# Ordering the tail of each feed-forward part, and a different reduction in the last norm

## The chip, the cores and the metric

The kernel runs on one core of one Trainium2 chip. The metric is the device time of one execution in microseconds (us). Engines in the profile: PE is TensorE's matmuls, PEld its weight loads, DVE is VectorE, ACT is ScalarE, POOL is GpSimd, SP issues the DMAs.

## The reference

Two layers of a bidirectional encoder on a sequence of 512 tokens of width 1024 in float32. Each layer has three sublayers, so six in all, numbered n = 0 to 5 here: feed-forward, mixer (a state-space scan in layer 0, attention in layer 1), feed-forward.

```python
for i in range(DEPTH):                                   # DEPTH = 2
    mods = (silu(c) @ ada_w[i] + ada_b[i]).reshape(b, 3, 3, D_MODEL)
    gate = lambda s: (1 + mods[:, s, 2])[:, None, :]
    y = swiglu(modulate(x, mods[:, 0]), w_gate[i, 0], w_up[i, 0], w_down[i, 0])
    x = layer_norm(ALPHA * x + 0.5 * gate(0) * y, ln_g[i, 0], ln_b[i, 0])
    y = mixer(modulate(x, mods[:, 1]))
    x = layer_norm(ALPHA * x + gate(1) * y, ln_g[i, 1], ln_b[i, 1])
    y = swiglu(modulate(x, mods[:, 2]), w_gate[i, 1], w_up[i, 1], w_down[i, 1])
    x = layer_norm(ALPHA * x + 0.5 * gate(2) * y, ln_g[i, 2], ln_b[i, 2])
# swiglu(u) = (silu(u @ w_gate) * (u @ w_up)) @ w_down, hidden width 2816
# layer_norm: (x - mean) / sqrt(var + 1e-5) * g + b over the 1024 features
```

## The kernel before

Activations lie transposed: 128 features on the partitions, 512 tokens along the free axis, so the residual `res[0..7]` is eight tiles. Each float32 value is held as a high part and a low part (`hi`/`lo`, `uh`/`ul` for activations, `wh`/`wl` for weights), and each product is three matmuls: high by high, high by low, low by high (`mm3`, L182). A weight tile is loaded as `raw` (512 KB, or 448 KB for a down tile of seven blocks), ACT copies it to `wh` (L123) and DVE subtracts to get `wl` (L126). There are five `raw` buffers in all during a feed-forward sublayer (four of the tag `raw` and one of the tag `raw5`), and all loads are issued from SP's queue at L99.

A feed-forward sublayer (`ffn`) splits its 22 hidden tiles into three parts of 8, 7 and 7. In a part, each hidden tile is computed, and then eight down units (`down_units`), one for each output tile, multiply the part's hidden tiles by a down weight (`wdn`) and add to the residual (`add_res`, L415, output `resid`). The hidden tiles come in two ways. Up to tile `first7` (10 for n = 0, 4 for the others) both projections are plain. From then on `seven` computes both by seven products of half blocks in place of eight (Strassen's scheme), from `input_forms` (sums of input halves) and `weight_forms` (sums of weight blocks, L543, L544 and L553). Its last product is `product(3, ...)` into the tile `mid`; behind it come, in a chain, L590 (`px`, DVE), L591 (`sg`, ACT: SiLU), L592 (`sg`, DVE), and `split_act`, which writes `hi` (L155, ACT) and `lo` (L156, DVE). A down unit multiplies the part's hidden tiles in their order, so the last hidden tile is needed by the last eighth (or seventh) of unit 0.

The modulation vectors (`mods`) are computed on DVE from another set of weights: a modulation unit (`ada_unit`, L207) loads one `raw` tile `in_adaw` and multiplies it by the conditioning vector with a running sum. Layer 0's units run in `ffn(0)`, layer 1's in `ffn(2)` and `ffn(3)`; `advance(stream, per[...])` issues two of them after each down unit in the first two parts of these three sublayers, one in the last part of `ffn(0)`, none in the last parts of the other two, and none at all in `ffn(5)`.

Nothing in the code fixes the order of the work of one engine except the data, the manual dependencies (`add_manual_dep` with `NOSYNC`: the one instruction stands behind the other on the engine's queue) and a scheduler, which plays the program forward when the kernel is built, and writes each engine's queue: of the instructions that are ready in its own model, the one that the program issues first goes first. On the chip each queue is then fixed.

The norm (`LN`) of the sublayers keeps two running sums on DVE, `sc` of the residual tiles and `ss` of their squares (`feed`, L326, L328, L329). `stats` reduces them over the partitions with matmuls by constant tiles (L335 for the broadcast mean in `mid`, L339 for mean and mean square by token), forms the variance on DVE (L344, L346, L349), takes the power -1/2 on POOL (L353), spreads the result by transposes (L276) and subtracts the mean from pairs of residual tiles (L357). `normalize` then scales; for the last norm, n = 5, it writes tile by tile on DVE (L367) and ACT (L370) and issues the output DMAs by pairs of tiles. The last four output tiles of the last part are done in two halves of 256 tokens, and the first half's normalization runs beside the second half's matmuls (`finish`).

Of the kernel before, what the change touches and what calls it, by code (L numbers as in the profile page):

```python
# [9 lines left out]
F32 = mybir.dt.float32  # L10
F32R = mybir.dt.float32r
AF = mybir.ActivationFunctionType
ALU = mybir.AluOpType

P = 128
# [31 lines left out]
def hybrid_trunk(tc, xT, cb, par, cst, adaw, wgu, wdn0, wdn1, wdn2, wdt, win, wso, wqk, wv, wao, dist_in, dtp, lam_in, out):  # L47
# [39 lines left out]
    def pc(c, n=1):  # L87
        return pars[:, c : c + n]


    fifth, at, last_load, hold_split = [None], [0], [None], [None]

    def load(src, n=1024):
        at[0] = (at[0] + 1) % 5
# [12 lines left out]
    def split(raw, where=None, home=None):  # L107

        n = raw.shape[-1]
        if where == "a":  # L110
            hi, lo = [], []
            for o in range(0, n, T):
                r = raw[:, o : o + T]
                h, l = big(F32R, "wah"), big(F32R, "wal")
                x = nc.scalar.activation(h, r, AF.Copy)
                y = nc.vector.tensor_tensor(out=l, in0=r, in1=h.bitcast(F32), op=ALU.subtract)
                for a, b in zip((x, y), behind):
                    tc.add_manual_dep(a.ins, b.ins.name, NOSYNC, reason="inputs before weights")
                hi.append(h)
                lo.append(l)  # L120
            return [(hi[c // T][:, c % T : c % T + P], lo[c // T][:, c % T : c % T + P]) for c in range(0, n, P)]
        hi, lo = ring(home)
        x = nc.scalar.activation(hi[:, :n], raw, AF.Copy)  # L123
        if hold_split[0] is not None:
            tc.add_manual_dep(x.ins, hold_split[0].ins.name, NOSYNC, reason="decay matrices first")
        nc.vector.tensor_tensor(out=lo[:, :n], in0=raw, in1=hi[:, :n].bitcast(F32), op=ALU.subtract)  # L126
        return Unit(hi, lo, n)

    def ring(home=None):
# [17 lines left out]

    def split_act(src, scale=None):
        hi, lo = big(F32R, "hi"), big(F32R, "lo")
        split_into(hi, lo, src, scale)  # L150
        return hi, lo

    def split_into(hi, lo, src, scale=None):
        if scale is None:
            x = nc.scalar.activation(hi, src, AF.Copy)  # L155
            y = nc.vector.tensor_tensor(out=lo, in0=src, in1=hi.bitcast(F32), op=ALU.subtract)  # L156
            return x, y
        else:
            nc.scalar.activation(hi, src, AF.Copy, scale=scale)
            nc.vector.scalar_tensor_tensor(  # L160
                out=lo, in0=src, scalar=scale, in1=hi.bitcast(F32), op0=ALU.mult, op1=ALU.subtract
            )
# [41 lines left out]

    def ada_unit(l, j):
        raw = load(adaw[l, j])
        nc.vector.scalar_tensor_tensor(  # L207
            out=raw, in0=raw, scalar=1.0, in1=cond, op0=ALU.mult, op1=ALU.mult,
            accum_out=mods[l][:, j : j + 1],
        )  # L210

    onep, shift, gvec, lnG, lnB, lnag, lnab = {}, {}, {}, {}, {}, {}, {}

# [84 lines left out]
    class LN:  # L298


        def __init__(self, n):
            self.n = n
            self.u = None

        def shift(self):

# [11 lines left out]
        def feed(self, d, a, b):  # L318
            z = res[d][:, a:b]
            if d == 0:  # L320
                self.sc = ap.tile([P, T], F32, tag="l", name="sc", bufs=3)
                self.ss = ap.tile([P, T], F32, tag="l", name="ss", bufs=3)
                nc.scalar.activation(self.ss[:, a:b], z, AF.Square)
                return
            sq = sp.tile([P, T], F32, tag="sq", name="sq")
            nc.scalar.activation(sq[:, a:b], z, AF.Square)  # L326
            c0 = res[0] if d == 1 else self.sc
            nc.vector.tensor_tensor(out=self.sc[:, a:b], in0=c0[:, a:b], in1=z, op=ALU.add)  # L328
            nc.vector.tensor_tensor(out=self.ss[:, a:b], in0=self.ss[:, a:b], in1=sq[:, a:b], op=ALU.add)  # L329

        def stats(self, a, b):
            n, m = self.n, (b - a) // P
            st = acc("ln")
            mb = acc("mid")[:, : b - a]
            nc.tensor.matmul(mb, lhsT=onesd, rhs=self.sc[:, a:b], start=True, stop=True)  # L335
            for q, c0 in enumerate((self.sc, self.ss)):
                for j in range(m):
                    o = a + j * P
                    nc.tensor.matmul(  # L339
                        st[:, q * m + j : q * m + j + 1], lhsT=c0[:, o : o + P], rhs=invd, start=True, stop=True  # L340
                    )
            rb = acc("ln")[:, : b - a]
            sv = sp.tile([P, 4], F32, tag="sv", name="sv")
            nc.vector.tensor_copy(sv[:, :m], st[:, :m])  # L344
            vr = sp.tile([P, 4], F32, tag="vr", name="vr")
            nc.vector.scalar_tensor_tensor(  # L346
                out=vr[:, :m], in0=sv[:, :m], scalar=-1.0, in1=sv[:, :m], op0=ALU.mult, op1=ALU.mult
            )
            ready = nc.vector.scalar_tensor_tensor(  # L349
                out=vr[:, :m], in0=st[:, m : 2 * m], scalar=EPS, in1=vr[:, :m], op0=ALU.add, op1=ALU.add  # L350
            )
            r = sp.tile([P, 4], F32, tag="rr", name="rr")
            nc.gpsimd.tensor_tensor(out=r[:, :m], in0=vr[:, :m], in1=mhalf[:, :m], op=ALU.pow)  # L353
            bcast_cols(rb, r[:, :m])
            for d in range(0, KT, 2):
                pair = resid[:, d : d + 2, a:b]
                x = nc.vector.tensor_tensor(out=pair, in0=pair, in1=two(mb), op=ALU.subtract)  # L357
                if d:
                    tc.add_manual_dep(x.ins, ready.ins.name, NOSYNC, reason="variance first")
            return rb  # L360

        def normalize(self, a, b, rb):
            n = self.n
            if n == 5:
                for d in range(KT):
                    t = res[d][:, a:b]
                    nc.vector.scalar_tensor_tensor(  # L367
                        out=t, in0=t, scalar=pc(C_LNG + n * 8 + d), in1=rb, op0=ALU.mult, op1=ALU.mult
                    )
                    nc.scalar.activation(t, t, AF.Identity, bias=pc(C_LNB + n * 8 + d))  # L370
                    if d % 2:
                        nc.sync.dma_start(
                            out[(d - 1) * P : (d + 1) * P, a:b].rearrange("(e p) t -> p e t", e=2),
                            resid[:, d - 1 : d + 1, a:b],
                        )
                    yield
                return
            if self.u is None:
# [217 lines left out]
    def ffn(n, stream=None, per=(0, 0, 0), pre=None, first7=FT):  # L596
# [10 lines left out]
        for pi, nf in enumerate(FPARTS):  # L607
# [36 lines left out]
            def mk(d):  # L644
                return lambda: [(d, split(load(wdn[pi][idx, d], nf * P)))]

            for _ in down_units(n, hs, [mk(d) for d in range(KT)], ln if pi == len(FPARTS) - 1 else None):
                advance(stream, per[1 if pi < 2 else 2])
            if pi == len(FPARTS) - 2:
                shifting = ln.shift()  # L650
        extra[0] = fifth[0] = None
# [746 lines left out]
```

## Time and profile before

| what | value |
|---|---|
| median of 3 runs | 2131.68 us (2131.55 to 2135.46) |
| the profiled execution: its time, its span | 2134.65 us, 2132.8 us |
| TensorE's granted clock in it | 0.997 |
| busy in the span: PE, PEld | 2099.9 us (98%), 1854.1 us (87%) |
| busy in the span: DVE, ACT, POOL | 1770.3 us (83%), 1093.8 us (51%), 180.6 us (8%) |
| mean traffic of the DMA engines | 141 GB/s |

In a timeline row stand the start in us from the span's start, the duration in us, engine, line of the kernel, operation, output and inputs by the program's names, shape and count, and in brackets the idle time of the engine just before it with what ended it. In a row of waits stand the engine and what waited, what it waited for, then the total in us, the number of times and the longest. In a row of stages stand the stretch, its length, the busy time of each engine, the clock, the DMA share and GB/s. In a row of groups stand the count, the busy time in us, the mean duration of one in ns, and the idle time before them.

### The profile page before, as it was taken

The page shows a single profiled execution, that of the slowest core. Times are in us where ns is not written, and L with a number is a line of the kernel's source. Part 1 is how long each engine was busy: PE and PEld are TensorE (multiplying, and loading weights), DVE is VectorE, ACT ScalarE, POOL GpSimd, SP SyncE. Part 2 cuts the span into 40 slices and gives each one's busy share as a digit, 9 for nine tenths or more (in the row PEclk, how much of TensorE's full clock was granted, in tenths as well). Part 3 has the DMA queues.
Part 4 walks back from the last instruction along what each step waited for, and adds up shares of the span by engine and source line. Part 5 has one row for each costly group of instructions (what it writes and reads, how often), then busy time and mean ns, then how long its engine had stood idle before and what let it go on. Part 6 is the DMA issues. An engine that isn't in the chain of part 4 may idle for free.

```text
span 2132.8 us, 34111 instructions
## 1 busy us (share of the span) xinstructions
PE 2099.9 (98%) x13234; PEld 1854.1 (87%) x13234; DVE 1770.3 (83%) x2932; ACT 1093.8 (51%) x1833; POOL 180.6 (8%) x258
## 2 busy tenths in 40 slices
PE   7999999999999999999999999999999999999998
PEld 6889899976777699899999989899988888989897
DVE  6979998677667898989988989997788889858796
ACT  5424354777656646343456434353866647424343
POOL 0000000056333400000000000000011100000000
PEclk9999999999999999999999999999999999999999
DMA  8863735375554352727343373723322322323231
GB/s 321 306 227 99 247 97 195 93 214 170 151 152 135 92 159 72 271 91 238 123 144 104 106 240 103 253 96 113 92 69 80 90 81 78 124 75 119 71 118 40
DMA packets 90274, 301.19 MB, mean 141 GB/s; under 512 B 10240, under 2 KB 13696, under 8 KB 90112
## 3 DMA queue, kind: packets, MB, share of 16 engines
q1 hardware_dynamic: 88576, 294.81, 42.6%
q0 software_dynamic: 1536, 4.20, 0.9%
q8 instruction: 104, 1.70, 0.3%
q14 instruction: 58, 0.48, 0.1%
HBM read 289.53 MB, written 5.24 MB: 138 GB/s over the span
## 4 chain that ended last, share of the span: by engine, by line
PE 85%; DVE 7%; DMA 2%; issue 2%; ACT 2%; POOL 1%; SPq 0%; POOLq 0%; ACTq 0%; DVEq 0%
PE acc L182 68%; PE mid L182 9%; PE mid L909 2%; PE mid L1142 1%; DVE raw L207 1%; PE ln L182 1%; DMA raw<-in_adaw 1%; DVE raw L553 1%; DVE wl L544 1%; DMA raw<-in_wdn 1%; PE ln L1164 1%; PE ln L847 0%; POOL E L899 0%; DVE wl L126 0%; PE ln L339 0%
## 5 line engine op out<-in xcount | busy, mean ns | idle before, releaser
L182 PE MATMUL acc<-hi,wh 128*128 128x256 f32 (+1 forms) x1568 | 522.0, 334 | 1.8 <-ACT hi L155 1.8
L182 PE MATMUL acc<-lo,wh 128*128 128x256 f32 (+1 forms) x1568 | 521.8, 333 | 0.6 <-DVE lo L156 0.6
L182 PE MATMUL acc<-hi,wl 128*128 128x256 f32 (+1 forms) x1568 | 520.6, 333 | 0.0
L182 PE MATMUL acc<-uh,wh 128*128 128x256 f32 (+1 forms) x1160 | 391.7, 339 | 0.0
L182 PE MATMUL acc<-uh,wl 128*128 128x256 f32 (+1 forms) x1160 | 386.6, 335 | 0.0
L182 PE MATMUL acc<-ul,wh 128*128 128x256 f32 (+1 forms) x1160 | 384.0, 335 | 0.0
L123 ACT ACTIVATE wh<-raw 128x1024 fp32r<-128x1024 f32 (+1 forms) x210 | 212.4, 1022 | 278.3 <-PE acc L182 109.6
L543 ACT ACTIVATE wh<-raw 128x1024 fp32r<-128x1024 f32 x198 | 209.3, 1059 | 255.2 <-DVE raw L553 115.2
L182 PEld LDWEIGHTS acc<-hi,wh 128*128 128x128 f32 x1568 | 295.9, 189 | 35.9 <-ACT hi L155 5.2
L182 PEld LDWEIGHTS acc<-lo,wh 128*128 128x128 f32 x1568 | 296.3, 189 | 31.0 <-DVE lo L156 2.4
L182 PEld LDWEIGHTS acc<-hi,wl 128*128 128x128 f32 x1568 | 296.0, 189 | 29.2
L126 DVE TENSOR_TENSOR wl<-raw,wh 128x1024 fp32r<-128x1024 f32 (+1 forms) x210 | 248.4, 1188 | 49.3 <-ACT wh L123 46.7
L544 DVE TENSOR_TENSOR wl<-raw,wh 128x1024 fp32r<-128x1024 f32 x198 | 240.9, 1219 | 22.5 <-ACT wh L543 21.0
L182 PEld LDWEIGHTS acc<-uh,wh 128*128 128x128 f32 x1160 | 219.1, 189 | 28.3 <-issue 6.4
L182 PEld LDWEIGHTS acc<-uh,wl 128*128 128x128 f32 x1160 | 219.1, 189 | 22.7 <-issue 0.4
L182 PEld LDWEIGHTS acc<-ul,wh 128*128 128x128 f32 x1160 | 217.5, 189 | 21.9 <-issue 0.6
L553 DVE TENSOR_TENSOR raw<-raw 128x512 f32<-128x512 f32 x264 | 181.3, 688 | 4.9
L207 DVE SCALAR_TENSOR_TENSOR raw<-raw,cond 128x1024 f32<-128x1024 f32 x144 | 173.7, 1218 | 10.5 <-DMA raw<-in_adaw 10.3
L415 DVE SCALAR_TENSOR_TENSOR resid<-acc,gv,resid 128x512 f32<-128x512 f32 (+1 forms) x156 | 104.5, 672 | 82.7 <-PE acc L182 82.1
L353 POOL TENSOR_TENSOR rr<-vr,mhalf 128x2 f32<-128x2 f32 x12 | 8.4, 698 | 1515.6 <-DVE vr L349 1515.6
L182 PE MATMUL mid<-uh,wh 128*128 128x256 f32 (+2 forms) x332 | 99.2, 301 | 0.5 <-DVE up L585 0.5
L182 PE MATMUL mid<-uh,wl 128*128 128x256 f32 (+2 forms) x332 | 99.0, 299 | 0.0
(268 smaller groups left out, 3926.0 us busy)
## 6 DMA issues: line engine op xcount, KB each, us to landing
raw<-in_wgu SPq DMA_DIRECT2D x176, 512.0 KB, 4.0
raw<-in_adaw SPq DMA_DIRECT2D x144, 512.0 KB, 4.7
raw<-in_wdn SPq DMA_DIRECT2D x64, 448.0 KB, 4.1
raw<-in_win SPq DMA_DIRECT2D x40, 512.0 KB, 4.0
raw<-in_wdn SPq DMA_DIRECT2D x32, 512.0 KB, 4.5
rw<-scr SPq DMA_DIRECT2D x32, 512.0 KB, 6.0
ch<-scr SPq DMA_DIRECT2D x32, 256.0 KB, 6.2
raw<-in_wso SPq DMA_DIRECT2D x16, 512.0 KB, 4.3
```

Source lines behind the costliest of these rows:

```text
L123: x = nc.scalar.activation(hi[:, :n], raw, AF.Copy)
L126: nc.vector.tensor_tensor(out=lo[:, :n], in0=raw, in1=hi[:, :n].bitcast(F32), op=ALU.subtract)
L182: last = nc.tensor.matmul(o, lhsT=a, rhs=b, start=start and j == 0, stop=j == len(pairs) - 1, skip_group_check=not start)
L207: nc.vector.scalar_tensor_tensor(out=raw, in0=raw, scalar=1.0, in1=cond, op0=ALU.mult, op1=ALU.mult, accum_out=mods[l][:, j : j + 1],)
L353: nc.gpsimd.tensor_tensor(out=r[:, :m], in0=vr[:, :m], in1=mhalf[:, :m], op=ALU.pow)
L415: nc.vector.scalar_tensor_tensor(out=res[d][:, a:b], in0=pd[:, a:b], scalar=gvec[n][:, d : d + 1], in1=res[d][:, a:b], op0=ALU.mult, op1=A ...
L543: nc.scalar.activation(x[0], r, AF.Copy)
L544: nc.vector.tensor_tensor(out=x[1], in0=r, in1=x[0].bitcast(F32), op=ALU.subtract)
L553: nc.vector.tensor_tensor(out=o, in0=x, in1=y, op=ALU.add)
L909: x = nc.tensor.matmul(py[hh * 64 : (hh + 1) * 64, cc], lhsT=lhs, rhs=rhs, start=k == 0, stop=k == 2)
L1142: nc.tensor.matmul(ss[m], lhsT=q[:, c], rhs=qks[h, 1][m], start=j == 0, stop=j == 1)
L1164: gated(nc.tensor.transpose(pw[:, k * P : (k + 1) * P], w[:, k * P : (k + 1) * P], ident))
```

## The change

It has three parts.

1. `split_act` remembers the two instructions of the latest activation split (`last_act`). In each of the three parts of each feed-forward sublayer, after down unit 0 has been issued, `part_end` is set to them until three units later: the ACT copy and the DVE subtraction of the splits of down units 1, 2 and 3, and the DVE multiplication of the modulation units issued after down units 0, 1 and 2, are ordered behind the two.
2. In the second half of the last norm (n = 5), the last residual tile is no longer added to `sc` and its square no longer to `ss`. TensorE adds them in the accumulation of the mean and of the token columns, each as a second matmul, with the column groups of the squares in a bank of their own and the broadcast mean's second matmul last.
3. In the same norm `normalize` multiplies pairs of residual tiles by the root in one DVE instruction, the gain moves into the ACT instruction (as its scale, with the bias as before), and in the second half the last three tiles get gain and bias on DVE (`tensor_scalar`).

```diff
+    last_act, part_end = [None], [None]
+
+    def behind_part(*xs):
+        for x, y in zip(xs, part_end[0] or ()):
+            tc.add_manual_dep(x.ins, y.ins.name, NOSYNC, reason="last activations of the part first")
...
     def split(raw, where=None, home=None):
...
-        nc.vector.tensor_tensor(out=lo[:, :n], in0=raw, in1=hi[:, :n].bitcast(F32), op=ALU.subtract)
+        y = nc.vector.tensor_tensor(out=lo[:, :n], in0=raw, in1=hi[:, :n].bitcast(F32), op=ALU.subtract)
+        behind_part(x, y)
         return Unit(hi, lo, n)
...
     def split_act(src, scale=None):
         hi, lo = big(F32R, "hi"), big(F32R, "lo")
-        split_into(hi, lo, src, scale)
+        last_act[0] = split_into(hi, lo, src, scale)
...
     def ada_unit(l, j):
         raw = load(adaw[l, j])
-        nc.vector.scalar_tensor_tensor(
+        x = nc.vector.scalar_tensor_tensor(
             out=raw, in0=raw, scalar=1.0, in1=cond, op0=ALU.mult, op1=ALU.mult,
             accum_out=mods[l][:, j : j + 1],
         )
+        if part_end[0]:
+            tc.add_manual_dep(x.ins, part_end[0][1].ins.name, NOSYNC, reason="last activations of the part first")
...
         def feed(self, d, a, b):
...
             nc.scalar.activation(sq[:, a:b], z, AF.Square)
+            if self.n == 5 and d == KT - 1 and a:
+                self.ends = (res[d], sq)
+                return
...
         def stats(self, a, b):
-            nc.tensor.matmul(mb, lhsT=onesd, rhs=self.sc[:, a:b], start=True, stop=True)
-            for q, c0 in enumerate((self.sc, self.ss)):
+            s2 = acc() if self.ends else st[:, m:]
+            cs, ss = ((x,) + self.ends[q : q + 1] for q, x in enumerate((self.sc, self.ss)))
+
+            def mean(i):
+                nc.tensor.matmul(mb, lhsT=onesd, rhs=cs[i][:, a:b], start=i == 0, stop=i == len(cs) - 1)
+
+            mean(0)
+            for to, c in ((st, cs), (s2, ss)):
+                prev = None
                 for j in range(m):
                     o = a + j * P
-                    nc.tensor.matmul(
-                        st[:, q * m + j : q * m + j + 1], lhsT=c0[:, o : o + P], rhs=invd, start=True, stop=True
-                    )
+                    for i, c0 in enumerate(c):
+                        x = nc.tensor.matmul(
+                            to[:, j : j + 1], lhsT=c0[:, o : o + P], rhs=invd, start=i == 0, stop=i == len(c) - 1
+                        )
+                        if prev is not None and self.ends:
+                            tc.add_manual_dep(x.ins, prev.ins.name, NOSYNC, reason="one accumulation group per bank")
+                        prev = x
+            if len(cs) > 1:
+                mean(1)
...
         def normalize(self, a, b, rb):
             if n == 5:
-                for d in range(KT):
-                    t = res[d][:, a:b]
-                    nc.vector.scalar_tensor_tensor(
-                        out=t, in0=t, scalar=pc(C_LNG + n * 8 + d), in1=rb, op0=ALU.mult, op1=ALU.mult
-                    )
-                    nc.scalar.activation(t, t, AF.Identity, bias=pc(C_LNB + n * 8 + d))
...
+                for d in range(0, KT, 2):
+                    pair = resid[:, d : d + 2, a:b]
+                    nc.vector.tensor_tensor(out=pair, in0=pair, in1=two(rb), op=ALU.mult)
+                    for e in range(2):
+                        t, G, B = res[d + e][:, a:b], pc(C_LNG + n * 8 + d + e), pc(C_LNB + n * 8 + d + e)
+                        if b == T and d + e > 4:
+                            nc.vector.tensor_scalar(out=t, in0=t, scalar1=G, scalar2=B, op0=ALU.mult, op1=ALU.add)
+                        else:
+                            nc.scalar.activation(t, t, AF.Identity, bias=B, scale=G)
+                    nc.sync.dma_start(out[d * P : (d + 2) * P, a:b].rearrange("(e p) t -> p e t", e=2), pair)
...
     def ffn(n, stream=None, per=(0, 0, 0), pre=None, first7=FT):
-            for _ in down_units(n, hs, [mk(d) for d in range(KT)], ln if pi == len(FPARTS) - 1 else None):
+            ends = last_act[0]
+            for i, _ in enumerate(down_units(n, hs, [mk(d) for d in range(KT)], ln if pi == len(FPARTS) - 1 else None)):
+                part_end[0] = ends if i < 3 else None
                 advance(stream, per[1 if pi < 2 else 2])
+            part_end[0] = None
```

More of the change, by code (lines that the diff above doesn't have):

```diff
@@ L303, in __init__ @@
             self.u = None
+            self.ends = ()
         def shift(self):
@@ L349, in stats @@
             ready = nc.vector.scalar_tensor_tensor(
-                out=vr[:, :m], in0=st[:, m : 2 * m], scalar=EPS, in1=vr[:, :m], op0=ALU.add, op1=ALU.add
+                out=vr[:, :m], in0=s2[:, :m], scalar=EPS, in1=vr[:, :m], op0=ALU.add, op1=ALU.add
             )
@@ L364, in normalize @@
             if n == 5:
-                for d in range(KT):
-                    t = res[d][:, a:b]
-                    nc.vector.scalar_tensor_tensor(
-                        out=t, in0=t, scalar=pc(C_LNG + n * 8 + d), in1=rb, op0=ALU.mult, op1=ALU.mult
-                    )
[L370 to L375, printed above, removed]
+                for d in range(0, KT, 2):
[8 more added lines that the diff above has]
+                    nc.sync.dma_start(out[d * P : (d + 2) * P, a:b].rearrange("(e p) t -> p e t", e=2), pair)
+                    yield
                     yield
```

## The prediction

> **What bounds the kernel now.** I read the page's busy row first, then the list of waits of TensorE, to see what a change at the ends of the feed-forward parts can win.
>
> ```profile
> PE 2099.9 (98%) x13234; PEld 1854.1 (87%) x13234; DVE 1770.3 (83%) x2932; ACT 1093.8 (51%) x1833; POOL 180.6 (8%) x258
> ...
> PE acc L182 <- ACT wah L115: 11.4, 1, 11.4
> ...
> PE acc L182 <- ACT hi L155: 1.8, 3, 0.8
> ...
> PE acc L182 <- DVE lo L156: 0.6, 1, 0.6
> ```
>
> TensorE is the bound: 98% of a span of 2132.8 us, and the largest wait (11.4 us) is the start, which the change leaves alone. The waits that the ties aim at are the last two rows: three times for `hi` (L155), once for `lo` (L156), 2.4 us in all. One of the four, with VectorE around it, shows the mechanism (timeline of DVE, of ACT, of PE; columns are start, duration, then the instruction):
>
> ```profile
> 871.18 1.21 DVE L126 TENSOR_TENSOR wl<-raw,wh 128x1024 fp32r<-128x1024 f32 x1
> ...
> 878.20 1.23 DVE L126 TENSOR_TENSOR wl<-raw,wh 128x1024 fp32r<-128x1024 f32 x1 [0.75 <-ACT wh L123]
> 879.34 1.22 DVE L207 SCALAR_TENSOR_TENSOR raw<-raw,cond 128x1024 f32<-128x1024 f32 x1
> 880.48 0.42 DVE L590 TENSOR_TENSOR px<-px,mid 128x256 f32<-128x256 f32 x1
> 880.82 1.22 DVE L126 TENSOR_TENSOR wl<-raw,wh 128x1024 fp32r<-128x1024 f32 x1
> 881.95 0.68 DVE L592 TENSOR_TENSOR sg<-sg,up 128x512 f32<-128x512 f32 x1
> 882.55 1.22 DVE L207 SCALAR_TENSOR_TENSOR raw<-raw,cond 128x1024 f32<-128x1024 f32 x1
> 883.70 0.68 DVE L156 TENSOR_TENSOR lo<-sg,hi 128x512 fp32r<-128x512 f32 x1
> 884.30 1.21 DVE L207 SCALAR_TENSOR_TENSOR raw<-raw,cond 128x1024 f32<-128x1024 f32 x1
> 885.45 0.74 DVE L415 SCALAR_TENSOR_TENSOR resid<-acc,gv,resid 128x512 f32<-128x512 f32 x1
> 886.11 1.21 DVE L126 TENSOR_TENSOR wl<-raw,wh 128x1024 fp32r<-128x1024 f32 x1
> ...
> 879.65 1.06 ACT L123 ACTIVATE wh<-raw 128x1024 fp32r<-128x1024 f32 x1 [0.54 <-DMA raw<-in_wdn]
> 880.93 0.42 ACT L591 ACTIVATE sg<-px 128x256 f32<-128x256 f32 x1 [0.22 <-DVE px L590]
> 882.67 0.63 ACT L155 ACTIVATE hi<-sg 128x512 fp32r<-128x512 f32 x1 [1.31 <-DVE sg L592]
> ...
> 878.60 0.28 PE L182 MATMUL mid<-uh,wl 128*128 128x256 f32 x1
> 878.72 0.39 PE L182 MATMUL acc<-hi,wl 128*128 128x512 f32 x1
> ...
> 882.38 0.40 PE L182 MATMUL acc<-hi,wh 128*128 128x512 f32 x1
> 882.62 0.39 PE L182 MATMUL acc<-lo,wh 128*128 128x512 f32 x1
> 883.35 0.50 PE L182 MATMUL acc<-hi,wh 128*128 128x512 f32 x1 [0.34 <-ACT hi L155]
> ```
>
> The last Strassen product of the part starts its last matmul at 878.60. Behind it come L590, L591, L592, L155, L156 one after the other, and two modulation units (L207) and two splits (L126) of the down weights stand among them on VectorE. Without them the five take 0.42 + 0.42 + 0.68 + 0.63 + 0.68 = 2.83 us and some 0.2 us of hand-offs: `lo` would end 0.3 + 3.0 = 3.3 us behind 878.60, at 881.9, in place of 884.4. So the diagnosis behind the ties is true: 2.5 us of delay on a short chain. TensorE hides all but 0.7 us of it under the first seven eighths of down unit 0.
>
> **What the ties win.** The rows call 2.4 us idle. From start to start 883.35 - 882.62 is 0.73 us where neighbours are 0.24 apart (882.62 - 882.38), so 0.49 are lost where the row says 0.34. Scaling 2.4 by 0.49/0.34 gives 3.5 us, which I take; the ends are 2.4 and 3.5. (The Trainium skill, "Perfetto Trace Analysis", section "Tensor Engine Instruction (MATMUL, LD_WEIGHTS)", says that a matmul's end is an estimate and only its start is observed; by that rule starts count and the win is 3.5, by the rows as they stand 2.4. These three rows agree with the rule.)
>
> **What the ties cost.** A part's splits 1 to 3 (`wh` behind the last `hi` on ACT, `wl` behind the last `lo` on DVE) and the modulation units that follow units 0, 1, 2 now all queue behind the chain. Nothing orders them among themselves but the program, in which the two units issued after down unit 0 come before split 1. The kernel's scheduler keeps to that order among what is ready: at 884.30 above it takes a modulation unit before a split whose `wh` was done at 880.71 (split 4, at 886.11). At the end of the last `lo` both units' data have long landed, while split 1's `wh` begins on ACT only behind `hi` and takes 1.06 us, longer than `lo`. So I expect DVE: `lo`, modulation unit, modulation unit, `wl` of split 1. From start to start a unit takes 1.14 (879.34 to 880.48), so `wl` ends 2 x 1.14 + 1.22 = 3.5 us after `lo`, and 0.74 later still if unit 0's `resid` (L415) slips in.
>
> When does TensorE need it? After 878.72 sixteen matmuls of 0.232 remain before the last eighth: its first at 882.43, the one with `lo` at 882.66, 0.76 us after `lo` would end. Then two of that unit and two of unit 1 (each 0.232), and the next needs `wl`: 0.93 later. The slack is 0.76 + 0.93 = 1.7 us, the delay 3.5: a new stall of 1.8 us in this part, where split 1 was finished at 872.4 before. A part of seven tiles has 21 matmuls a unit in place of 24: 0.7 us less, stall 2.5.
>
> Five parts end on Strassen products and have two units after each down unit: layer 0's first feed-forward part 2 of 3 (seven tiles), parts 1 (eight) and 2 (seven) of the sublayers n=2 and n=3. That is 2 x 1.8 + 3 x 2.5 = 11.1 us. The last part of n=0 has one unit per down unit: 1.14 + 1.22 - 1.0 = 1.4. Ends for these six: nothing if split 1 goes first, and 6 x 3.5 = 21 if there is no slack.
>
> The first part of n=0 is of another kind: there the last `split_act` is not an activation but the second half of `input_forms`, which is needed only later:
>
> ```profile
> 103.46 0.68 DVE L631 TENSOR_TENSOR h<-sg,acc 128x512 f32<-128x512 f32 x1
> ...
> 106.20 1.22 DVE L126 TENSOR_TENSOR wl<-raw,wh 128x1024 fp32r<-128x1024 f32 x1
> ...
> 112.22 0.69 DVE L156 TENSOR_TENSOR lo<-fb,hi 128x512 fp32r<-128x512 f32 x1
> ```
>
> From `h` (103.46) to the end of that `lo` (112.91) are 9.45 us, in which two units, one split and one `resid` take some 4.3. Taken out, `lo` ends at 108.6; units and split 1 to 112.1. TensorE's unit 1 starts at about 108.1 and needs `wl` 0.5 later: 3.5 us, or less if `h` moves up too. I take 3.0 (ends 0 and 4.2, with `resid`).
>
> Parts without modulation units (last part of n=2 and n=3, all of n=5) queue only split 1: `wh` ends 1.06 after `hi`, `wl` 1.2 later, 1.6 after `lo`, against 1.0 to 1.7 of slack: I take 0 (ends 0 and 0.6 x 5 = 3). What covers them is that slack alone.
>
> **Behind the stalls: VectorE and the loads.**
>
> ```profile
> 865.00:884.00 19.00, 18.66 (x133) 17.21 (x133) 18.11 (x30) 8.54 (x12) 0.00 (x0) 1.00 0.75 244
> 884.00:925.00 41.00, 41.00 (x190) 33.93 (x189) 34.81 (x52) 11.00 (x12) 0.00 (x0) 1.00 0.65 234
> ...
> 861.47 3.61 SPq L99 DMA_DIRECT2D raw<-in_wdn  x2
> ...
> 898.11 6.16 SPq L99 DMA_DIRECT2D raw<-in_wgu  x5
> ```
>
> (Columns of the first two rows: length, busy PE, PEld, DVE, ACT, POOL, clock, DMA share, GB/s.) DVE is full ahead of the chain (18.1 of 19 us) because units and splits run ahead; that work, four units and two splits in that window (7.3 us) and three more units before it (3.6), moves behind. The down stage has 41 - 34.8 = 6.2 us idle for these 10.9. Loads wait likewise: all five `raw` buffers hold tied data, SP's queue stops on the next buffer, and loads that ran from 861 on start after the first unit is through. In place of 898 the next part's `in_wgu` go perhaps 10 us later. The eight down units of 24 matmuls last 44.5 us on TensorE, to about 927, so I put this at 0, with 8 us (two for each of four following parts) as the other end.
>
> **The last norm.** Its tail, in order:
>
> ```profile
> 2120.15 0.28 PE L182 MATMUL acc<-hi,wl 128*128 128x256 f32 x1
> 2121.72 0.70 PE L335 MATMUL mid<-sc,onesd 128*128 128x256 f32 x2 [1.30 <-DVE sc L328]
> 2122.62 0.58 PE L339 MATMUL ln<-invd,ss 128*128 128x1 f32 x4
> ...
> 2124.10 0.16 DVE L349 SCALAR_TENSOR_TENSOR vr<-ln,vr 128x2 f32<-128x2 f32 x1
> 2124.18 1.87 DVE L357 TENSOR_TENSOR resid<-resid,mid 128x512 f32<-128x512 f32 x3
> 2125.97 3.22 DVE L367 SCALAR_TENSOR_TENSOR resid<-resid,pars,ln 128x256 f32<-128x256 f32 x8
> 2126.48 3.30 ACT L370 ACTIVATE resid<-resid,pars 128x256 f32<-128x256 f32 x8 [3.54 <-DVE resid L367]
> ...
> L339 PE MATMUL ln<-invd,ss 128*128 128x1 f32 x48 | 6.9, 247 | 0.0
> L382 DVE TENSOR_TENSOR resid<-resid,ln 128x512 f32<-128x512 f32 x40 | 25.9, 678 | 0.2 <-PE ln L276 0.2
> L706 DVE TENSOR_SCALAR E<-E 128x256 f32<-128x256 f32 x1 | 0.3, 294 | 1.4 <-ACT E L705 1.4
> ```
>
> The two adds (L328, L329) go; TensorE gets five extra products instead (four columns, one mean), and the first mean and its columns run under `add_res`. A column's piece follows the one before by (0.58 - 0.247)/3 = 0.11 us and there are now 16; with the last matmul done at 2120.43 the second mean ends at 2120.43 + 0.7 + 16 x 0.11 + 0.7 = 2123.6 at the latest. I take 2123.5, so the four subtractions of 0.6 end at 2125.9 (before: 2126.05) and the variance is off the path. Then four pair products of about 0.6 (L382 is the same shape) in place of 3.22 us, and three `tensor_scalar` of 0.29 on DVE: 2125.9 + 2.4 + 0.9 = 2129.2, where ACT ended at 2126.48 + 3.30 = 2129.78 before. Gain 0.6 us (ends 0 and 1.3). Pairs in the first half run beside the second half's matmuls: nothing. POOL's root and SP's output queue keep their order.
>
> **Sum.** 11.1 + 1.4 + 3.0 + 0 + 0 - 3.5 - 0.6 = +11.4 us. The profiled execution took 2134.65 us (span 2132.8 and 1.85 around it), 3.0 above the median of 2131.68; the same step on the median gives 2143.1. About 0.2% (4.3 us) is what a measurement can tell from no change.
>
> **Rivals.**
> 1. *Split 1 keeps its place.* If `wl` of split 1 stands ahead of the units, or the chain ends over 1.8 us earlier than I work out, the new stall is zero and the win stays: -3.5 - 0.6 = -4.1, 2127.6 us, at the edge of faster. For it: the short chain, and that TensorE's waits are real. Against it: the order at 884.30. It decides from a delay under 1.7 us, one unit instead of two (2.4) being already too much. (The Trainium skill, "Perfetto Trace Analysis", section "Optimization Strategy", would have one find the gaps on the busiest engine and make what they wait for start sooner; by that rule this rival wins. The rows at 882.62 and 883.35 bear out the gap, not that nothing takes its place.)
> 2. *Wash.* One unit ahead of the split in most parts, or the units already behind: six times 0.5 to 0.7 us lost against 4.1 won, 2131 to 2135.
> 3. *The stage behind is late as well.* DVE cannot make up 10.9 us in 6.2 of idle time, and the next part's first Strassen product waits for its forms: 8 us more, 2151.
>
> **How the numbers follow.** Forecast 0.50, rival 1 0.16, rival 2 0.20, rival 3 0.14. Faster by over 0.2%: 0.16 (rival 1 with any further win); within: 0.20; slower: 0.50 + 0.14 = 0.64. The forecast's own range is 2136.5 to 2149; the 8-in-10 range reaches from rival 1 to rival 3, 2127 to 2151.
>
> **What would show it.** In the changed trace the waits of PE for `hi` and `lo` in these parts are gone; new waits of `acc` L182 for `wl` L126 stand at the start of down unit 1, about 2 us each; DVE shows two L207 rows between the last L156 and the first L126. DVE is idle before the chain, and `in_wgu` are issued later behind 884. The last ACT row of the kernel ends before DVE's. If `wl` follows `lo` at once, or PE's waits for `wl` sum to under 4 us, the forecast is wrong.

## The result and the profile after

The changed kernel took 2156.85 us (median of 5 runs, 2155.84 to 2160.74), the kernel before 2132.12 us: a ratio of 1.0115, 95% interval 1.0104 to 1.0126, so 24.7 us slower. The profiled execution took 2155.84 us, its span is 21.2 us longer than that of before.

From the page of the changed kernel, the busy row:

```profile
PE 2106.8 (98%) x13244; PEld 1859.0 (86%) x13244; DVE 1771.9 (82%) x2925; ACT 1092.4 (51%) x1830; POOL 176.4 (8%) x258
```

VectorE has as much work as before (1771.9 for 1770.3 us); the work was moved, not added. TensorE's list of waits (total, times, longest):

```profile
PE acc L188 <- DVE wl L131: 9.5, 6, 3.1
PE mid L351 <- DVE sc L340: 3.1, 2, 2.3
...
PE acc L188 <- ACT wh L568: 2.1, 3, 0.9
```

The waits for `hi` and `lo` at the parts' ends are gone, as the ties want it. In their place stand waits for `wl` of split 1 (L131), for the sums of a norm (L340) and for the weight forms of the next part's Strassen products (L568). This part of n=2 shows the first kind (DVE, then PE):

```profile
895.65 0.69 DVE L162 TENSOR_TENSOR lo<-sg,hi 128x512 fp32r<-128x512 f32 x1 [0.70 <-ACT hi L161]
896.26 1.22 DVE L213 SCALAR_TENSOR_TENSOR raw<-raw,cond 128x1024 f32<-128x1024 f32 x1
...
897.41 1.22 DVE L213 SCALAR_TENSOR_TENSOR raw<-raw,cond 128x1024 f32<-128x1024 f32 x1
...
898.55 1.22 DVE L131 TENSOR_TENSOR wl<-raw,wh 128x1024 fp32r<-128x1024 f32 x1
...
893.04 0.28 PE L188 MATMUL mid<-uh,wl 128*128 128x256 f32 x1
893.15 0.40 PE L188 MATMUL acc<-hi,wh 128*128 128x512 f32 x1
...
899.83 0.50 PE L188 MATMUL acc<-hi,wl 128*128 128x512 f32 x1 [0.57 <-DVE wl L131]
```

`lo`, two modulation units, `wl`, and TensorE released with the end of `wl`: the order that was forecast, instruction by instruction.

Where the time went is read by following one mark through both traces: the additions into `resid` (L415 before, L440 after) that close each part. Their time after minus before, as steps from mark to mark:

| stretch | step, us |
|---|---|
| n=0, first part | +7.2 |
| n=0, second and last part up to the norm | +2.0 |
| norm of n=0 and start of the scan | +6.2 |
| n=1, n=4 | +0.1 |
| n=2 (three parts) | +4.7 |
| n=3 (three parts) | +2.7 |
| n=5 (three parts: -0.35, -0.45, -0.37) | -1.2 |
| last norm's tail | -0.56 |

They sum to the 21.2 us of the spans. A single step is uncertain by about 1 us: in f4 below n=3 has no ties, and two of its parts differ from before by -0.95 and -1.18.

The first part of n=0 in the changed trace (timeline of DVE, then of PE):

```profile
109.18 0.69 DVE L162 TENSOR_TENSOR lo<-fb,hi 128x512 fp32r<-128x512 f32 x1
109.79 1.22 DVE L213 SCALAR_TENSOR_TENSOR raw<-raw,cond 128x1024 f32<-128x1024 f32 x1
...
110.93 0.75 DVE L440 SCALAR_TENSOR_TENSOR resid<-acc,gv,resid 128x512 f32<-128x512 f32 x1
111.60 1.22 DVE L213 SCALAR_TENSOR_TENSOR raw<-raw,cond 128x1024 f32<-128x1024 f32 x1
...
112.74 1.22 DVE L131 TENSOR_TENSOR wl<-raw,wh 128x1024 fp32r<-128x1024 f32 x1
...
110.15 0.50 PE L188 MATMUL acc<-hi,wh 128*128 128x512 f32 x1 [0.39 <-ACT wh L128]
110.48 0.40 PE L188 MATMUL acc<-lo,wh 128*128 128x512 f32 x1
114.01 0.71 PE L188 MATMUL acc<-hi,wl 128*128 128x512 f32 x1 [3.13 <-DVE wl L131]
114.53 0.63 PE L188 MATMUL acc<-hi,wh 128*128 128x512 f32 x1
114.95 0.63 PE L188 MATMUL acc<-lo,wh 128*128 128x512 f32 x1
```

Two things cost here. By starts TensorE loses 3.3 us before 114.01 and 0.56 before 110.15. And then seven matmuls start 0.425 apart (114.53 to 114.95 and so on) where neighbours elsewhere are 0.23 apart: 1.4 us more. The granted clock (the column behind POOL's busy time) says the same of this stretch:

```profile
114.00:117.90 3.90, 3.89 (x10) 3.07 (x11) 3.90 (x6) 1.06 (x1) 0.00 (x0) 0.56 0.94 266
```

The norm of n=0, in the same windows of both kernels (those of after moved by its lag of 8.5 us). Before:

```profile
350.00:375.00 25.00, 25.00 (x205) 24.56 (x204) 19.98 (x43) 11.29 (x24) 0.70 (x1) 1.00 0.19 65
375.00:385.00 10.00, 10.00 (x86) 9.93 (x85) 8.82 (x17) 5.97 (x12) 0.86 (x2) 1.00 0.30 105
```

After:

```profile
358.50:383.50 25.00, 23.64 (x188) 22.77 (x186) 23.71 (x49) 11.36 (x22) 0.70 (x1) 1.00 0.47 158
383.50:393.50 10.00, 7.20 (x58) 6.81 (x59) 9.74 (x23) 6.14 (x12) 0.85 (x2) 1.00 0.32 107
```

VectorE (third busy column) has 3.7 us more to do in the first window and is full in the second; TensorE stands still for 4.2 us of 35 where it had no gap. The timeline after shows with what:

```profile
369.40 1.22 DVE L213 SCALAR_TENSOR_TENSOR raw<-raw,cond 128x1024 f32<-128x1024 f32 x1
...
371.60 1.22 DVE L213 SCALAR_TENSOR_TENSOR raw<-raw,cond 128x1024 f32<-128x1024 f32 x1
...
384.95 0.70 PE L351 MATMUL mid<-sc,onesd 128*128 128x256 f32 x2 [2.33 <-DVE sc L340]
```

Modulation units that were held back stand among the norm's sums, and the norm's first product waits 2.33 us for `sc`.

### The profile page after: what moved, and what is told of

It is laid out like the page before. It is cut to its first block, busy times and chain, and to the rows that moved or that the text cites. A ratio compares the mean times of both kernels' runs of the same rounds, so it can differ in the third digit from the quotient of the medians.

```text
span 2154.0 us, 34062 instructions
## 1 busy us (share of the span) xinstructions
PE 2106.8 (98%) x13244; PEld 1859.0 (86%) x13244; DVE 1771.9 (82%) x2925; ACT 1092.4 (51%) x1830; POOL 176.4 (8%) x258
## 4 chain that ended last, share of the span: by engine, by line
PE 87%; DVE 5%; issue 3%; DMA 2%; ACT 2%; POOL 1%; SPq 0%; POOLq 0%; DVEq 0%; ACTq 0%
PE acc L188 68%; PE mid L188 11%; PE mid L937 2%; DVE raw L213 2%; PE mid L1170 1%; PE ln L188 1%; DMA raw<-in_adaw 1%; PE ln L1192 1%; DMA raw<-in_wdn 1%; PE ln L875 0%; DVE wl L131 0%; PE ln L284 0%; DMA raw<-in_wgu 0%; PE ln L359 0%; ACT wh L568 0%
## 5 line engine op out<-in xcount | busy, mean ns | idle before, releaser
L568 ACT ACTIVATE wh<-raw 128x1024 fp32r<-128x1024 f32 x198 | 207.0, 1057 | 191.9 <-DVE raw L578 107.6
L131 DVE TENSOR_TENSOR wl<-raw,wh 128x1024 fp32r<-128x1024 f32 (+1 forms) x210 | 246.7, 1187 | 41.9 <-ACT wh L128 37.9
L440 DVE SCALAR_TENSOR_TENSOR resid<-acc,gv,resid 128x512 f32<-128x512 f32 (+1 forms) x156 | 104.5, 672 | 60.7 <-PE acc L188 59.9
```

Source lines behind the costliest of these rows:

```text
L131: y = nc.vector.tensor_tensor(out=lo[:, :n], in0=raw, in1=hi[:, :n].bitcast(F32), op=ALU.subtract)
L440: nc.vector.scalar_tensor_tensor(out=res[d][:, a:b], in0=pd[:, a:b], scalar=gvec[n][:, d : d + 1], in1=res[d][:, a:b], op0=ALU.mult, op1=A ...
L568: nc.scalar.activation(x[0], r, AF.Copy)
```

## The experiments

All times are medians of the runs of one comparison, with the ratio to the kernel before run beside them. The first four take the change apart.

**e1, norm alone.**

```
-                part_end[0] = ends if i < 3 else None
+                part_end[0] = None
```

> The change's two edits of the last norm alone, no ties. Theory (all of the loss comes from the ties, the norm wins 0.5 us): 2131.5 us, within 0.2% of before, and the stretch from the last product of the kernel to the end of the span is 0.4 to 0.7 us shorter than before's 12.4 us. Rival (the norm's extra matmuls or its DVE step cost something): that stretch is not shorter.

Measured 2133.33 us, ratio 1.0001 (0.9992 to 1.0011). The step of the tail is -0.55 us. The edits of the norm are no part of the loss.

**e2, ties of the splits alone** (units untied, norm as before).

```
     def ada_unit(l, j):
...
-        if part_end[0]:
-            tc.add_manual_dep(x.ins, part_end[0][1].ins.name, ...)
```

> Only splits 1 to 3 of the down units are tied; modulation units and the norm as before. Theory (what costs is two modulation units standing ahead of split 1 on VectorE, which needs both ties, and VectorE's lost run-ahead): the units still run early, split 1 follows the last lo at once, so stalls at down unit 1 are under 1 us each and the time is 2130 to 2137 us. Rival (tying the splits is what makes the weights late): at least 12 of the 24.7 us stay, 2144 us or more.

Measured 2143.24 us, 1.0049 (1.0034 to 1.0064): more than the theory allowed, and just short of the rival. Its waits:

```profile
PE mid L188 <- DVE up L608: 3.3, 3, 1.2
...
PE acc L188 <- ACT wh L128: 2.6, 1, 2.6
```

The free units now run ahead of the chain and delay `up` in n=2 and n=3 (steps of +3.4 and +2.8 in their second parts, of which their last parts take back 2.0 and 1.4); in the first part of n=0 (+5.0) the split's `wh`, on ScalarE, waits behind the input forms' `hi`.

**e3, ties of the units alone** (splits untied, norm as before).

```
-        behind_part(x, y)
```

> Only the modulation units are tied; splits and the norm as before. Theory: split 1 is finished ahead of the chain as before, so PE has no wait for wl at down unit 1, TensorE's waits for the last hi and lo shrink, and what is left of the loss is VectorE's lateness in the stage behind (first Strassen products of the next part, norm of n=0): 2133 to 2143 us. Rival (the units' tie alone carries the loss): 2150 us or more.

Measured 2141.93 us, 1.0050 (1.0033 to 1.0067): inside what was expected, with no wait for `wl` at unit 1. So units held back cost even where split 1 is free. e2 and e3 lose 10.4 and 9.1 us, 19.5 of the 24.7.

**e4, no ties in n=0.**

```
-                part_end[0] = ends if i < 3 else None
+                part_end[0] = ends if i < 3 and n > 0 else None
```

> The whole change, but no ties in the first feed-forward sublayer (n=0). Theory by the add_res marks of the two traces (15.4 us of the loss have come by the first add_res of the scan, n=1): 2157 - 15.4 = 2141.5 us, 2139 to 2144; PE shows no wait of over 2.5 us and no run of 512-column matmuls 0.42 us apart after the start. Rival (what is lost in n=0 is slack that the later stages lose anyway): 2150 us or more.

Measured 2139.25 us, 1.0031 (1.0020 to 1.0043), as expected: with n=0 free 6.4 us of the 24.7 are left, so n=0 carries some 18 us of the loss, most of it in its first part and its norm.

**e5, first part of n=0 tied to its last hidden tile.**

```
-            ends = last_act[0]
+            ends = last_act[0] if f > first7 else hidden_end
```

(`hidden_end` is `last_act[0]` after the split of the last hidden tile.)

> The whole change, but in the first part of n=0 the splits and units are tied behind the split of the last hidden tile (the last activation proper) and not behind the second half of the input forms. Theory (the first part's 7.2 us come from being tied to the wrong instruction, whose end lies 9 us behind the last hidden tile: a wait of 3.3 us and a run of matmuls at half rate behind it): the step of the first part falls from 7.2 to between 1 and 3 us, the matmuls behind unit 1's start are 0.23 apart again, and the time is 2151 to 2154, where the whole change has 2156.85. Rival (the first part is late whatever it is tied to, since units and splits together are too much for VectorE there): the step stays at 5 us or more, 2155 to 2158.

Measured 2154.27 us, 1.0101 (1.0084 to 1.0118). The step fell to 4.4 us and the total to 2154.27, both between what the theory and the rival gave, and the matmuls at half rate, which the theory had gone, stayed. TensorE now waited for unit 1's weights (DVE, then PE):

```profile
109.88 1.21 DVE L131 TENSOR_TENSOR wl<-raw,wh 128x1024 fp32r<-128x1024 f32 x1
...
111.20 0.50 PE L188 MATMUL acc<-hi,wh 128*128 128x512 f32 x1 [2.69 <-ACT wh L128]
...
112.26 0.63 PE L188 MATMUL acc<-hi,wl 128*128 128x512 f32 x1
```

The list names the `wh` that ended beside it, but split 1's own `wl` ended only at 111.09: two units, the last steps of the forms and a `resid` still stood ahead of it. Being tied to the forms was a part of the 7.2 us, not all of it.

**e6, next split ahead of the units.**

```
+            def make(d):
+                return split(load(wdn[pi][idx, d], nf * P))
+            ready = {}
...
-                return lambda: [(d, split(load(wdn[pi][idx, d], nf * P)))]
+                return lambda: [(d, ready.pop(d) if d in ready else make(d))]
...
+                if i + 1 < KT:
+                    ready[i + 1] = make(i + 1)
                 advance(stream, per[1 if pi < 2 else 2])
```

> The whole change, but the load and split of the next down unit are issued in the program ahead of the modulation units that follow a down unit, so that split 1 stands ahead of both units on VectorE. Theory (the order among the tied instructions makes the waits for wl, 9.5 us in five waits by the list): these waits fall under 3 us in all; what VectorE has to make up later (the norm of n=0, the first products of the next parts) stays, so that 2140 to 2148 is expected. Rival (the order does not matter, everything tied comes too late together): no change, 2155 to 2158.

Measured 2158.32 us, 1.0115 (1.0100 to 1.0131). The theory's waits went, its time did not come:

```profile
PE mid L351 <- DVE sc L340: 5.6, 3, 2.5
PE acc L188 <- ACT px L601: 4.3, 9, 0.5
...
PE acc L188 <- DVE wl L131: 1.0, 1, 1.0
```

The wait for `wl` fell from 9.5 to 1.0 us; what was won at unit 1 came back between the second part of n=0 and its norm (+7.7 for +2.0) and at that norm (step +8.5 for +6.2). Behind the norm's waits the matmuls were again at half rate:

```profile
372.60:380.30 7.70, 7.70 (x38) 7.65 (x39) 5.91 (x15) 2.93 (x5) 0.70 (x1) 0.56 0.22 68
```

In all, 52 matmuls of 128x256 stand 0.21 apart there in place of 0.12, so some 5 us of this execution's +25.4 us are half rate, against 1.4 of the changed kernel's +21.2: without them both lose about 20 us. So the order at unit 1, on which the prediction's largest term stood, decides only where the loss appears. (The edit also moves the loads of the later down units ahead of those of the modulation units; it is not the order at unit 1 alone.)

**e7, last part of n=0 untied.**

```
-                part_end[0] = ends if i < 3 else None
+                part_end[0] = ends if i < 3 and not (n == 0 and pi == 2) else None
```

> The whole change without the ties in the last part of n=0, the one before that sublayer's norm and the start of the scan, where the lag against the kernel before grows by 6.2 us. Theory (that part's own units, tied, stand among the additions of the norm): the step there falls under 2 us and the time is about 2150. Rival (the lateness is carried in from the two parts before): the step stays near 6 us and the time at 2155 to 2158.

Measured 2153.14 us, 1.0093 (1.0078 to 1.0108). The step at the norm went from +6.2 to -0.5, as the theory says, but the stretches before it rose (+7.0 from the second part to the norm, where the changed kernel has +2.0), with a wait of 1.82 us for the same sums inside them:

```profile
375.56 0.67 PE L351 MATMUL mid<-sc,onesd 128*128 128x256 f32 x2 [1.82 <-DVE sc L340]
```

Both were partly right: that part's own units reach the norm, and lateness is carried in too.

**e8, ties from down unit 1 on.**

```
-                part_end[0] = ends if i < 3 else None
+                part_end[0] = ends if 0 < i < 4 else None
```

> Ties only from down unit 1 on: splits 2 to 4 and the units after down units 1 to 3 are tied, split 1 and the units after down unit 0 are free as before. Theory (the loss is the queue behind the chain: two units and split 1 in the slack of one down unit; and split 1 is the only one needed at once): no wait for wl at unit 1, less to make up on VectorE, 2131 to 2138. Rival (any tie makes VectorE late at the next stage, whichever split is free): the first products of the next parts and the norm of n=0 still lose, 2142 to 2150.

Measured 2133.10 us, 1.0010 (1.0000 to 1.0020), inside the theory's range and below the rival's. With split 1 and two units free to run ahead of the chain, the whole loss is gone but for at most 0.2%. The windows around that part of n=2 (19 us before the chain's end, 41 of the down stage, 20 behind it; each moved by its kernel's lag) show where VectorE's work goes. Changed kernel:

```profile
880.45:899.45 19.00, 18.81 (x133) 17.28 (x131) 11.78 (x21) 4.94 (x9) 0.00 (x0) 1.00 0.24 80
899.45:940.45 41.00, 40.62 (x185) 33.55 (x186) 37.76 (x58) 12.02 (x13) 0.00 (x0) 1.00 0.84 300
940.45:960.45 20.00, 20.00 (x169) 19.86 (x168) 19.41 (x31) 9.59 (x14) 0.00 (x0) 1.00 0.42 136
```

e8:

```profile
863.61:882.61 19.00, 19.00 (x136) 17.86 (x136) 14.44 (x23) 6.43 (x10) 0.00 (x0) 1.00 0.39 128
...
923.61:943.61 20.00, 19.80 (x164) 19.47 (x164) 16.65 (x27) 9.46 (x14) 0.00 (x0) 1.00 0.33 106
```

Before, the last of them:

```profile
925.00:945.00 20.00, 20.00 (x167) 19.70 (x166) 15.05 (x24) 7.97 (x13) 0.00 (x0) 1.00 0.25 79
```

VectorE's work ahead of the chain was 18.11 us before, 14.44 in e8, 11.78 with the change. With the change 6.3 us were taken out; 3.0 more stand in the down stage (37.76 for 34.81) and 4.4 more in the stage behind it (19.41 for 15.05), about 1 us more than left the first window, since work was held back ahead of it too. In e8 the stage behind has 16.65. These windows show the debt, not its price: in the stage behind this part TensorE is busy for 20.00 of 20 us even with the change (19.80 in e8), and what e8 saves here is the wait at unit 1.

The price behind the parts falls due after the second parts of n=0, n=2 and n=3, and there the loads come first. The last part of n=3, before (SP's queue), then with the change (SP's queue, ACT, PE):

```profile
1364.90 6.93 SPq L99 DMA_DIRECT2D raw<-in_wgu  x5
```

```profile
1396.59 13.40 SPq L104 DMA_DIRECT2D raw<-in_wgu  x6
...
1401.90 1.06 ACT L568 ACTIVATE wh<-raw 128x1024 fp32r<-128x1024 f32 x1 [3.26 <-DMA raw<-in_wgu]
...
1409.80 0.39 PE L188 MATMUL acc<-hi,wh 128*128 128x256 f32 x1 [0.86 <-ACT wh L568]
```

The weights of this part are issued 31.7 us later than before, where the whole kernel lags by some 21: about 11 us late. ScalarE waits for them, and the weight forms made from them release TensorE at 1409.80. In e8 the same loads start at 1371.58, some 7 us late, and two short waits for forms are left (0.4 and 0.7 us by the rows).

**f1, the wait filled.** Fourteen matmuls that nobody reads, between down units 0 and 1 of the first part.

```
+                if n == 0 and pi == 0 and i == 0:
...
+                    for j in range(14):
...
+                        y = nc.tensor.matmul(po, lhsT=onesn, rhs=hs[j % 7][0], start=j % 7 == 0, stop=j % 7 == 6)
...
```

> The whole change, and in the first part of n=0, between down units 0 and 1, fourteen matmuls of 128x512 whose result nobody reads, so that TensorE works (14 x 0.23 = 3.2 us) where it waits 3.3 us for wl in the changed kernel. All instructions of the change stay where they are. Theory (the seven matmuls 0.425 apart behind that wait, 1.4 us lost, and the granted clock of 0.56 in that window come from TensorE standing still before them): behind the filled wait the matmuls are 0.23 apart, the granted clock is 1.00, and the step of the first part falls from 7.2 to about 5.8 us. Rival (the matmuls are slow because what they read is late or because VectorE and the transfers are busy then): seven slow matmuls again, step 7 us or more. The time of the whole kernel: 2154 to 2157 by the theory, 2156 to 2160 by the rival.

Measured 2156.22 us, 1.0105 (1.0091 to 1.0119). In place of the seven slow matmuls (timeline of PE, then the window):

```profile
113.10 0.50 PE L188 MATMUL acc<-hi,wl 128*128 128x512 f32 x1 [0.53 <-DVE wl L131]
113.44 0.40 PE L188 MATMUL acc<-hi,wh 128*128 128x512 f32 x1
113.68 0.39 PE L188 MATMUL acc<-lo,wh 128*128 128x512 f32 x1
```

```profile
114.00:118.00 4.00, 4.00 (x20) 3.29 (x19) 4.00 (x8) 0.65 (x1) 0.00 (x0) 1.00 0.95 365
```

Starts 0.24 apart and a granted clock of 1.00, with VectorE and the transfers as busy as before (4.00 of 4, DMA share 0.95): that speaks for TensorE's own standing still as what halves its rate, and the rival falls. It is one execution; e7, in which the same wait of 3.13 us was not filled, shows the half rate again (13 matmuls from 113.33 on). The step fell to 4.7 us, more than forecast, since `wl` also came 0.9 us earlier. The time of the whole kernel lies in both ranges; it gained little, as in the profiled execution the matmuls behind the wait at 231.4 us and in the norm of n=0 ran at half rate, 3.3 us in all.

**f2 and f3, small units**, in the changed kernel and in the one before.

```
-            out=raw, in0=raw, scalar=1.0, in1=cond, op0=ALU.mult, op1=ALU.mult,
+            out=raw[:, :64], in0=raw[:, :64], scalar=1.0, in1=cond[:, :64], op0=ALU.mult, op1=ALU.mult,
```

> The whole change, with every modulation unit reading 64 of its 1024 columns (0.1 us or so on VectorE in place of 1.2; the loads stay whole). To be compared with the same edit on the kernel before, run beside it. Theory (the loss is VectorE's backlog: what the ties hold back has to be done in the down stage and the stage behind it, where VectorE is full): with the units small, the change costs 5 us or less against its partner. Rival (the loss is the loads: tied units hold the raw buffers, and the next loads are issued late): the difference stays at 15 us or more, as the loads are untouched.

> The kernel before, with every modulation unit reading 64 of its 1024 columns; partner of the run with the same edit on the changed kernel. Both theories: TensorE is the bound and VectorE had been hidden, so 2126 to 2133.

Measured: f2 2142.47 us, 1.0038 (1.0026 to 1.0050); f3 2142.66 us, 1.0040 (1.0026 to 1.0054). Both leave out 960 of the 1024 columns of each modulation sum. Between the two the change costs nothing, where whole units cost 24.7 us. But f3 missed what was expected of it by 10 us. With cheap units the splits run further ahead and stand before the chain:

```profile
PE mid L182 <- DVE up L585: 4.9, 5, 1.8
```

So the pair is not clean. What can be read is the step from the changed kernel to f2: 15.3 of its 24.7 us go with the units' time on VectorE, and the 9.4 us left are near the 10.4 of e2, in which only splits are tied. The rival of late loads does not fall: the last parts of n=0, n=2 and n=3 still lose 3.4, 2.8 and 2.6 us in f2 (0.3, 1.7 and 2.0 with whole units), and `in_wgu` of the last part of n=3 start at 1383.03, 18.1 us later than before at a lag of 7.5, so as late as with the change.

**f4, ties in n=5 alone, with the norm.**

```
-                part_end[0] = ends if i < 3 else None
+                part_end[0] = ends if n == 5 and i < 3 else None
```

> The edits of the last norm, and ties in the sublayer n=5 alone, where no modulation units are left and the changed kernel won 0.35, 0.45 and 0.37 us in the three parts. Theory (these parts and the tail win whatever stands ahead): 0.55 + 1.17 = 1.7 us faster than before, a ratio of 0.9992, at the edge of what can be measured. Rival (the three steps belong to the lateness carried into them): 0.5 us faster, ratio 0.9998.

Measured 2130.82 us, 0.9985 (0.9976 to 0.9994): 0.15% faster than the kernel before, the theory's ratio inside the interval and the rival's outside. By the medians it is 2.3 us below e8, so the ties of the parts with units may still cost a little there. The three parts of n=5 show -0.40, -0.46 and -0.36 us, the tail -0.55.

## Why the prediction was wrong

The direction and the mechanism at unit 1 held, the size was half: +11.4 us forecast, +24.7 measured, beyond the range's upper end of 2151. What failed is the term put at 0 for VectorE and the loads behind the stalls, and the size of the first part of n=0.

- *Gone waits for `hi` and `lo`*: right. By starts they had cost 3.1 us (0.9, 0.5, 0.8, 0.9), of which the forecast made 3.5; as a gain they cannot be seen alone, as the new costs lie in the same stretches. The 1.2 us won in n=5 are something else: before, the list names none of these waits there, and what is gone are steps of TensorE that were 0.05 to 0.1 us too long near the parts' ends, about 1 us in all.
- *Tail of the last norm, -0.6*: right, 0.53 to 0.57 in the ten kernels with these edits. VectorE now ends the kernel, and the variance is off the path (the spread root ends at 2146.53, before VectorE is through with its subtractions):

```profile
2145.84 0.69 PE L284 MATMUL ln<-csts,rr 128*128 128x128 f32 x2 [1.13 <-POOL rr L378]
2146.65 2.47 DVE L392 TENSOR_TENSOR resid<-resid,ln 128x512 f32<-128x512 f32 x4
2147.37 2.57 ACT L398 ACTIVATE resid<-resid,pars 128x256 f32<-128x256 f32 x5 [3.67 <-DVE resid L392]
2149.04 1.05 DVE L396 TENSOR_SCALAR resid<-resid,pars 128x256 f32<-128x256 f32 x3
```

- *Stall at unit 1, 11.1 + 1.4*: right in kind, too large. By starts the five stalls are 2.0, 0.7, 1.8, 0.6 and 1.9, in all 7.1 us; the last part of n=0 shows none. The delay of `wl` was as worked out (3.4 us behind the end of `lo` at 896.34; 3.5 forecast). The slack was not: the forecast took from the trace of before that a few matmuls of down unit 0 are done ahead of the last Strassen product. In the changed trace unit 0 begins behind it (893.15), so 26 matmuls run before `wl` is needed and not 21: 1.1 us more slack.
- *First part of n=0, 3.0*: the step that failed first, 7.2. The order on VectorE and a wait near the measured 3.3 us were forecast, `resid` ahead of `wl` only as the upper end; not in the sum were 0.56 us for `wh` and the half rate behind the wait, 1.4 us. The remaining 1.9 us stay open: kernels without ties in this part differ from before by +0.4 (e1), -0.3 (e4) and +1.2 (f4), so a part of them may be chance.
- *VectorE and the loads behind, 0*: the step that failed most. It was put at 0 because a down stage lasts 44 us, and it cost 10.5 us in two places. The norm of n=0, which rival 3 did not name, lost 6.2 us: units that were held back stand among its sums on VectorE. The first Strassen products of the parts behind lost 4.3 us (six waits of 0.5 to 1.0 by starts, none there before); that was rival 3, put at 8 us for four following parts. The prediction had the numbers for both: 10.9 us of work into 6.2 us of idle time (12.1 us with split 1, at 871.18, which the count left out), of which the down stage took 3.0, and `in_wgu` perhaps 10 us later, which is what came (11 us in n=3). What it missed is that the slack is not the length of the stage: the weight forms need another 6 to 8 us from the landing of their loads. e6 shows what kind of cost it is: a backlog, of which the order at unit 1 chooses the place and not the size. How much of the 4.3 us is late loads and how much VectorE's own lateness in making the forms, no run separates.
- *Parts without units, 0*: no cost at unit 1 came, as forecast; the 1.2 us won in n=5 were not in the sum.

By these sizes the terms come to 7.1 (stalls) + 7.2 + 6.2 + 4.3 - 3.1 - 1.2 - 0.6 = 19.9 us, against +21.2 of the spans, with single steps uncertain by about 1 us. That the forecast plus the first part (+4.2) and the norm (+6.2) alone gives 21.8 is luck: the stalls came out 5.4 us below the forecast's 12.5, and the products behind, not in the sum, cost 4.3. The gap from the spans to the medians' 24.7 is that the profiled execution of before (2134.65) lies 2.5 us above its median and that of after (2155.84) 1.0 below.

## What to carry to other kernels

Work held back from a nearly full engine is a debt: before tying it behind a chain, count what it comes to and ask not whether the next stage has idle time on average but which instruction of the next stages will be late, and which loads wait for the buffers that the held work keeps. Hold back only what the next consumer does not need at once, and leave the engine some of the work to do while the chain waits for others (e8, at most 0.2%; e3, 9 us). A wait of two or three microseconds on TensorE may be priced with its echo, the matmuls at half rate behind it.

## What the runs showed of the hardware

TensorE can run at half rate behind a wait. After waits of 2.0 to 3.3 us (by starts) five to thirteen matmuls of 128x512 stood 0.425 us apart in place of 0.23, for 2 to 5.5 us, at a granted clock of 0.50 to 0.57 in such windows; it cost 1.0 to 2.6 us each time, and once the wait was filled it was gone (f1). It differs from execution to execution: behind the wait of 2.0 us at 231.68 the changed kernel lost nothing, while e5 lost 1.4 us behind the same one. In f2 it followed even waits of 1.6 and 1.2 us by starts, in the norms of n=0 and n=1; the first of them:

```profile
371.00:374.00 3.00, 3.00 (x16) 3.00 (x16) 2.97 (x8) 0.42 (x1) 0.70 (x1) 0.50 0.24 94
```

It is not the ties' own doing: the kernel before has one such stretch, in the scan, behind a wait of 2.50 us:

```profile
497.05:500.45 3.40, 3.33 (x10) 2.77 (x11) 1.80 (x3) 2.44 (x7) 0.72 (x1) 0.50 0.34 94
```

The ties make waits of that length, and with them more such stretches. The page's row of clocks, in 54 us slices, shows nines throughout; a window of a few microseconds is needed.

The Trainium skill, "TensorE: Matmul & The Clock Gate", section "Part 1: The HAM clock gate (the "warmup" mystery)", says that an idle window of about 3.4 us puts TensorE on half its clock and that the window runs freely. The half rate, and that it comes and goes between executions, agree with these traces; but here waits of 1.2 to 2.0 us were enough.
